# The first layer's normalisation of a two-layer trunk moved ahead of its first products

## The chip, the cores and the metric

One core of a Trainium2 chip runs one program for the whole trunk. TensorE is called PE below, VectorE DVE, ScalarE ACT, GpSimd POOL, and SyncE's queue, from which all the transfers are issued, SP. The metric is the device time of one execution in microseconds, as the median over several runs.

## What is computed

Two layers over 1024 positions of width 1024. Each normalises its input, scales and shifts it by a modulation that is worked out from a condition vector, multiplies it by one wide input matrix, runs three mixers over slices of the product, and merges their gated outputs. The change touches the lines down to `proj`, in the first layer.

```python
def rms_norm(x, g):
    x32 = x.astype(jnp.float32)
    y = x32 * lax.rsqrt(jnp.mean(x32 * x32, axis=-1, keepdims=True) + NORM_EPS)
    return (y * g).astype(x.dtype)
...
def hybrid_layer(x, c_act, positions, norm_g, w_ada, b_ada, w_in, ...):
    mod = c_act @ w_ada + b_ada
    shift, scale, gate = jnp.split(mod[:, None, :], 3, axis=-1)
    h = rms_norm(x, norm_g) * (1.0 + scale) + shift
    proj = h @ w_in
    pool_u, pool_g, q, k, v, ret_g, rw, rw_g, gate_logits = jnp.split(proj, points, axis=-1)
    o_pool = causal_pool_mixer(pool_u, pool_w, pool_scale) * jax.nn.silu(pool_g)
    o_ret = retention(q, k, v, positions, ret_norm_g) * jax.nn.silu(ret_g)
    o_rwkv = rwkv7_time_mix(rw, ...) * jax.nn.silu(rw_g)
    y = jnp.einsum('btnw,nwd->btnd', jnp.stack([o_pool, o_ret, o_rwkv], axis=2), w_branch)
    merged = jnp.sum(jax.nn.sigmoid(gate_logits.reshape(B, T, N_BRANCHES, D)) * y, axis=2)
    return x + gate * (merged @ w_out)
```

## The kernel before

The sequence stands on the free axis in two halves of 512 positions, `h` = 0 and 1. The width of 1024 stands on the partitions in eight row blocks, `kt` = 0 to 7. So the input is sixteen tiles of 128x512, `xin[h][kt]`. A product at full precision is made of three fast ones: both operands are split into a rounded part and a remainder (`hhi` and `hlo` for the inputs, `wh` and `wl`, or `wbig`, for the weights), and `mm1` issues hi by hi, lo by hi and hi by lo into one accumulator. A product of 128x512 of this kind is called a dense matmul below. One output tile of 128 columns over both halves takes 48 of them.

The modulation is 24 columns of 128 values: 0 to 7 are the shift, 8 to 15 the scale, 16 to 23 the gate. `ada` works out a group of them (`ADA`): for each of the eight row blocks of `w_ada` DVE multiplies a wide tile by one value of the condition and adds it to an accumulator in SBUF (L216, L218). PE then sums over the partitions with matmuls against a column of ones (`adaps`), and DVE adds the bias. For a scale group it also makes `acoef`, which is the norm's gain times one plus the scale. Before the change, the groups are 2, 2 and 4 columns of scale, then 4 and 4 of shift, then the gate.

The start is written out by hand, in one block in which the order of instructions on PE, DVE, ACT and POOL is that of the text (L1228 to L1343). It works in two passes:

1. The first three output tiles (`FIRST`: the lora columns, `k` and `r` of the first head pair) are multiplied from inputs that are only scaled (`scaled`: x times `acoef`, split into hi and lo). Their six accumulators stand in PSUM (`acc6`). They take 16 blocks of nine dense matmuls (`mms(h, kt)`), 144 in all. Beside that, ACT squares the inputs (`sq`), POOL sums the squares, and `rstd_task` makes the norm's factor for each position and spreads it over the partitions (`rbc`). The six products are multiplied by that factor when they leave PSUM (`first_raw`). What the shift contributes to them is worked out from a second load of the raw weights on DVE (`shift_bias`), and added at the end (`first_evac`).
2. For all further output tiles the inputs themselves are multiplied by the factor (`normed`, in place, on POOL and DVE), scaled and shifted (`shifted`), and split once more into the same hi and lo tiles. In this block the first two further output tiles, `v` of the first head pair and one of the pooling mixer, are multiplied as these tiles become ready.

After the block, a planner with its own clock (`wprep`, `pump`, `advance`) fills PE with the input tiles of the other mixers and places the steps of the mixers among them. The first matmul of a mixer's task is `lw` (L729), of the first head pair of the RWKV mixer. `FIRST` and `v` of that head pair must be out of PSUM before that task is added (L1045).

Transfers wait in SP's order; tiles of 256 KB follow one another with eight of them in flight.

Of the kernel before, what the change touches and what calls it, by code (L numbers as in the profile page):

```python
# [17 lines left out]
P = 128  # L18
# [71 lines left out]
def trunk_kernel(ctx, tc, xT, cvec, pos, vecs, consts, w_ada, w_all, pool_w, lora_w, out):  # L90
# [113 lines left out]
    def ada(l, g, slot_, gap=2200, acc_=t_lt, ws=None):  # L204
        c, n, _ = ADA[g]
        W_ = n * P
        acc = acc_("ada_acc")[:, 0:W_]
        late = ws is None
        ws = [] if late else ws
        for kt in range(NKT):  # L210
            i, o = divmod(kt * W_, HF)
            if late and o == 0:
                ada_load(l, g, slot_, ws, min(i + 2, 2 * n) - len(ws))
            w = ws[i][:, o : o + W_]
            if kt == 0:
                nc.vector.tensor_scalar_mul(acc, w, cact[:, 0:1])  # L216
            else:
                nc.vector.scalar_tensor_tensor(acc, w, cact[:, kt : kt + 1], acc, op0=ALU.mult, op1=ALU.add)  # L218
# [6 lines left out]
        o = VEC["b_ada"]  # L225
        nc.vector.tensor_tensor(mod[l][:, c : c + n], ps[:, 0:n], vec[l][:, o + c : o + c + n], op=ALU.add)
        if c >= 16:
            nc.vector.tensor_scalar_mul(mod[l][:, c : c + n], mod[l][:, c : c + n], 0.5)
        if 8 <= c < 16:
            o = VEC["norm_g"] + c - 8  # L230
            nc.vector.scalar_tensor_tensor(
                acoef[l][:, c - 8 : c - 8 + n], mod[l][:, c : c + n], 1.0, vec[l][:, o : o + n],
                op0=ALU.add, op1=ALU.mult,
            )
        yield
# [349 lines left out]
    def affine_hi(l, kt, x, res, eng=None):  # L585
        nc.scalar.activation(
            x, x, AF.Identity, bias=mod[l][:, kt : kt + 1], scale=acoef[l][:, kt : kt + 1]
# [381 lines left out]
    def shift_evac(l, mui, ps, h, am_prev, dst):  # L969
        o = VEC["mu_k"] + mui  # L970
        mu = vec[l][:, o : o + 1]
        keep = pin if pinned[0] else lambda i: i
        keep(nc.scalar.activation(dst[:, 1:HF], ps[:, 0 : HF - 1], AF.Copy, scale=mu))
        if h == 0:
            keep(nc.gpsimd.memset(dst[:, 0:1], 0.0))
# [26 lines left out]
    pinned = [False]  # L1002
# [18 lines left out]
    def evac_steps(item, ps, h, bias=None):  # L1021
        l, st, ams, lw = L_
        kind = item[0]
        if kind == "lora":
            d = mo("lt")
            ams["lora"] = shift_evac(l, 12, ps, h, ams.get("lora"), d)
            if bias:
                yield bias(d, h, 12)
# [4 lines left out]
        elif kind in ("k", "r", "v"):  # L1033
# [8 lines left out]
            if bias:  # L1042
                yield bias(d, h, mui)
# [45 lines left out]
    def evac(*a):  # L1089
        run(evac_steps(*a))  # L1090

# [12 lines left out]
    ssum = [None, None]  # L1104
    rbc = [[], []]
    wbig = []
    wparts = [[], [], []]
    acc6 = []

    sqs = {}  # L1110
# [7 lines left out]
    def sq(h, kt):  # L1118
        sqs[h, kt] = (mo if kt else t_cs)("sq")
        nc.scalar.square(sqs[h, kt], xin[h][kt])  # L1120
        if kt == 0:
            ssum[h] = sqs[h, kt]
        else:
            nc.gpsimd.tensor_tensor(ssum[h], ssum[h], sqs[h, kt], op=ALU.add)
# [17 lines left out]
    def scaled(h, *kts):  # L1142
        for kt in kts:
            x, a = xin[h][kt], acoef[0][:, kt : kt + 1]
            hi, lo = hb("hhi"), hb("hlo")
            nc.scalar.activation(hi, x, AF.Copy, scale=a)
            nc.vector.scalar_tensor_tensor(lo, x, a, hi.bitcast(F32), op0=ALU.mult, op1=ALU.subtract)
            h_cur[h].append((hi, lo))

# [4 lines left out]

    def rstd_copy(h):
        rb = t_lt("rbs")
        nc.scalar.copy(rb, rbc[h][0])
        rbc[h].append(rb)

    first_steps = []  # L1160

    raws = {}

    def first_raw(h, *tiles):
        for i in tiles:
            raws[h, i] = mo("raw")
            nc.vector.tensor_tensor(raws[h, i], acc6[h][i], rbc[h][1], op=ALU.mult)

    def first_evac(h, *tiles):
        for i in tiles:  # L1170
            st = evac_steps(FIRST[i], raws[h, i], h, lambda d, hh, mui, i=i: (d, hh, mui, i))
            first_steps.append((st, next(st)))

    def normed(eng, h, *kts):
        for kt in kts:
            eng.tensor_tensor(xin[h][kt], xin[h][kt], rbc[h][1], op=ALU.mult)

    def shifted(h, *kts):
        for kt in kts:
            x = xin[h][kt]  # L1180
            hi, lo = h_cur[h][kt]
            b, a = mod[0][:, kt : kt + 1], acoef[0][:, kt : kt + 1]
            if kt % 2 and (kt >= 4 or h):
                nc.scalar.activation(hi, x, AF.Identity, bias=b, scale=a)
                nc.vector.tensor_scalar(x, x, a, b, op0=ALU.mult, op1=ALU.add)
            else:
                nc.scalar.activation(x, x, AF.Identity, bias=b, scale=a)
                nc.scalar.copy(hi, x)
            nc.vector.tensor_tensor(lo, x, hi.bitcast(F32), op=ALU.subtract)

    def shift_bias():
        ws = [[None, None] for _ in range(3)]
        for i in range(3):
            for j in range(2):
                ws[i][j] = wada_slot("wraw")
                nc.sync.dma_start(out=ws[i][j], in_=w_all[0, i, j])
        yield
        acc = t_cs("bacc")
        for i in range(3):
            ai = acc[:, i * P : (i + 1) * P]  # L1200
            for kt in range(NKT):
                w = ws[i][kt // 4][:, kt % 4 * P : kt % 4 * P + P]
                b = mod[0][:, kt : kt + 1]
                if kt == 0:
                    nc.vector.tensor_scalar_mul(ai, w, b)
                else:
                    nc.vector.scalar_tensor_tensor(ai, w, b, ai, op0=ALU.mult, op1=ALU.add)
        ps = mx("bias")
        for i in range(3):
            mmul(ps[:, i : i + 1], acc[:, i * P : (i + 1) * P], ones)  # L1210
        b = t_cs("bias")[:, 0:3]
        nc.vector.tensor_copy(b, ps[:, 0:3])
        for st, (d, h, mui, i) in first_steps:
            bi = b[:, i : i + 1]
            if h == 0:
                nc.vector.scalar_tensor_tensor(
                    d[:, 0:1], bi, omu[0][:, mui : mui + 1], d[:, 0:1], op0=ALU.mult, op1=ALU.add
                )
                nc.scalar.activation(d[:, 1:HF], d[:, 1:HF], AF.Identity, bias=bi)
            else:  # L1220
                nc.scalar.activation(d, d, AF.Identity, bias=bi)
            run(st)
# [5 lines left out]
    with tc.manual_schedule(engines={ET.PE, ET.DVE, ET.Activation, ET.Pool}):  # L1228
        acc6.append([acc_ps() for _ in range(3)])
        acc6.append([ps_c.tile([P, HF], F32, tag=t, name=nm("acc"), bufs=n) for t, n in (("cy", 2), ("cy", 2), ("ch", 1))])  # L1230
        aw = [[] for _ in range(5)]
        gs = [ada(0, g, None, acc_=t_vp if g == 4 else t_lt, ws=aw[g]) for g in range(5)]
# [3 lines left out]

        aload(0, 4)
        nc.sync.dma_start(out=vec[0], in_=vecs[0])
        wdma(0, 0)
        wsp(0, 0)  # L1240
        xdma(0, 0, 1)
        wdma(0, 1, 2)
        xdma(1, 0, 1)
        aload(1, 4)
        xdma(0, 2, 3)
        xdma(1, 2, 3)
        steps(gs[0], 9)
        derive(0)
        scaled(0, 0)
        wsp(0, 1)  # L1250
        steps(gs[1], 3)
        scaled(0, 1)
        wsp(0, 2)
        steps(gs[1], 5)
        mms(0, 0, 1)
        sq(0, 0)
        sq(0, 1)
        steps(gs[1], 1)
        scaled(1, 0, 1)
        sq(1, 0)  # L1260
        sq(1, 1)
        mms(1, 0, 1)
        aload(2, 8)
        for h in range(2):
            for kt in (2, 3):
                steps(gs[2], 2)
                scaled(h, kt)
                sq(h, kt)
        mms(0, 2, 3)
        wdma(1, 0, 1, 2)  # L1270
        xdma(0, 4, 5, 6, 7)
        nc.sync.dma_start(out=cst, in_=consts[:, 0 : CST["bone"]])
        xdma(1, 4, 5, 6, 7)
        wsp(1, 0, 1, 2)
        mms(1, 2)
        steps(gs[2], 1)
        mms(1, 3)
        for tag in ("wh", "wl"):
            for _ in range(3):
                w = wp.tile([P, HF], F32, tag=tag, name=nm("wada"), bufs=3)  # L1280
                ada_load(0, 3, lambda _: w, aw[3], 1)
        aload(3, 2)
        for kt in range(4, 8):
            sq(0, kt)
            scaled(0, kt)
            mms(0, kt)
        for kt in range(4, 8):
            sq(1, kt)
            scaled(1, kt)
            steps(gs[3], 2)  # L1290
        wprep(True)
        aload(4, 8)
        r0 = rstd_task([ssum[0]], rbc[0])
        r1 = rstd_task([ssum[1]], rbc[1])
        mms(1, 4)
        next(r0)
# [26 lines left out]
        for i in range(2):  # L1323
            pss[i, 0] = acc_ps()
# [330 lines left out]
```

## Time and profile before

| | |
|---|---|
| median of 3 runs | 2525.3 us (2524.45 to 2537.53) |
| the profiled execution | 2538.0 us, span 2536.3 us |
| mean granted TensorE clock | 0.971 |
| PE, DVE, ACT, POOL busy | 95%, 55%, 31%, 33% of the span |
| moved by DMA | 225 MB, mean 89 GB/s |

A row of the timeline gives the start in the span, the busy time, the engine, the line and operation, and the tiles as written by read, with what ended the idle time before it in brackets. Rows of groups give the total and the mean duration of one. The duration of a matmul is longer than the step from one to the next, as they are pipelined; so the step between starts is what counts. Matmuls on fp32 operands appear twice in the trace, since each is made in two passes.

### The profile page before, as it was taken

Reading aid. Unit: us, or ns where it says so; the run is one execution under the profiler, and the core shown is the slowest. Engines: PE = TensorE matmul, PEld = TensorE weight load, DVE = VectorE, ACT = ScalarE, POOL = GpSimd, SP = SyncE. Lnnn points to the kernel's source line nnn. Section 1 sums busy time; section 2 is a strip of 40 time slices with the busy share of each in tenths; the row PEclk is TensorE's granted clock in tenths of the full one; section 3 lists DMA queues with packets and bytes.
Section 4 is the critical chain, followed back from the end, with each engine's and each line's share of the span. In section 5 each row is a group of like instructions: output and inputs, shape, how many; then the busy total and the mean of one; then the engine's idle time right before and its main releaser. Section 6 shows DMA issues by size and latency. Waiting matters only on the chain. (4 is left out here: it accounts for less than half of the span.)

```text
span 2536.3 us, 34936 instructions
## 1 busy us (share of the span) xinstructions
PE 2417.6 (95%) x13318; PEld 1995.5 (79%) x13318; DVE 1394.0 (55%) x2588; ACT 796.6 (31%) x1482; POOL 847.6 (33%) x729
## 2 busy tenths in 40 slices
PE   6889999999899999999999999999999999999998
PEld 4677887787788788877878787788878778787888
DVE  7886358357547935267455735844744663412344
ACT  4642232233224222212353223223322322221243
POOL 5522223133133332364452222322313322236441
PEclk9799999999999999999999999999999989999999
DMA  6222112011112413666541211211211121354342
GB/s 229 76 88 71 38 38 84 28 40 64 55 35 83 133 47 130 189 212 195 170 126 34 80 34 38 68 41 35 86 45 38 60 79 51 117 158 122 105 152 76
DMA packets 125080, 225.25 MB, mean 89 GB/s; under 512 B 14192, under 2 KB 17520, under 8 KB 124912
## 3 DMA queue, kind: packets, MB, share of 16 engines
q1 hardware_dynamic: 124912, 223.01, 27.8%
q8 instruction: 105, 1.72, 0.3%
q14 instruction: 63, 0.52, 0.1%
HBM read 176.03 MB, written 46.92 MB: 88 GB/s over the span
## 5 line engine op out<-in xcount | busy, mean ns | idle before, releaser
L513 POOL TENSOR_TENSOR wl<-wr,wh 128x512 fp32r<-128x512 f32 x338 | 450.3, 1333 | 1220.2 <-ACT wh L512 1123.0
L394 PE MATMUL acc<-hhi,wh 128*128 128x512 f32 x1968 | 799.5, 406 | 29.1 <-DVE k L981 29.1
L394 PE MATMUL acc<-hlo,wh 128*128 128x512 f32 x1968 | 801.7, 407 | 0.0
L394 PE MATMUL acc<-hhi,wl 128*128 128x512 f32 x1968 | 799.2, 406 | 0.0
L394 PEld LDWEIGHTS acc<-hhi,wh 128*128 128x128 f32 x1968 | 377.7, 192 | 100.4 <-DVE k L981 31.6
L512 ACT CAST wh<-wr 128x512 fp32r<-128x512 f32 x338 | 209.3, 619 | 734.3 <-PE acc L394 476.0
L394 PEld LDWEIGHTS acc<-hhi,wl 128*128 128x128 f32 x1968 | 377.6, 192 | 68.8 <-issue 2.2
L394 PEld LDWEIGHTS acc<-hlo,wh 128*128 128x128 f32 x1968 | 377.2, 192 | 68.8 <-issue 1.3
L394 PE MATMUL acc<-olo,wh 128*128 128x512 f32 x384 | 154.2, 402 | 5.8 <-POOL olo L513 5.8
L394 PE MATMUL acc<-oG,wh 128*128 128x512 f32 x384 | 153.1, 400 | 3.5 <-ACT oG L512 1.7
L394 PE MATMUL acc<-oG,wl 128*128 128x512 f32 x384 | 152.5, 398 | 0.0
L936 DVE SCALAR_TENSOR_TENSOR S<-ch,pc,SP 64x64 f32<-64x64 f32 x256 | 72.5, 283 | 105.0 <-PE ch L394 98.5
L925 DVE TENSOR_TENSOR xst<-cy,MT 64x128 f32<-64x128 f32 x128 | 36.1, 282 | 168.7 <-PE cy L394 168.4
L922 ACT ACTIVATE SP<-S,pc 128x128 f32<-128x128 f32 x128 | 51.4, 402 | 179.1 <-DVE S L936 175.1
L858 DVE TENSOR_TENSOR tm<-MT 64x30 f32<-64x30 f32 (+14 forms) x240 | 100.2, 417 | 7.6
L864 DVE TENSOR_TENSOR MT<-MT,tm 64x30 f32<-64x30 f32 (+14 forms) x240 | 95.2, 397 | 7.8
L931 DVE COPY Z<-ch 64x128 f32<-64x128 f32 x128 | 36.1, 282 | 112.3 <-PE ch L394 111.7
L394 PEld LDWEIGHTS acc<-olo,wh 128*128 128x128 f32 x384 | 73.2, 191 | 24.6 <-POOL olo L513 8.9
L394 PEld LDWEIGHTS acc<-oG,wh 128*128 128x128 f32 x384 | 73.2, 191 | 22.7 <-ACT oG L512 2.9
L1482 DVE SCALAR_TENSOR_TENSOR gs<-gs,acc 128x512 f32<-128x512 f32 x64 | 43.5, 682 | 85.8 <-PE acc L394 74.6
L218 DVE SCALAR_TENSOR_TENSOR ada_acc<-wada,cact,ada_acc 128x512 f32<-128x512 f32 (+1 forms) x68 | 70.0, 1029 | 31.9 <-DMA wada<-in_w_ada 31.0
L394 PEld LDWEIGHTS acc<-oG,wl 128*128 128x128 f32 x384 | 73.6, 192 | 16.6
(292 smaller groups left out, 3825.3 us busy)
## 6 DMA issues: line engine op xcount, KB each, us to landing
wr<-in_w_all SPq DMA_DIRECT2D x364, 256.0 KB, 2.7
gd<-gsg SPq DMA_DIRECT2D x80, 256.0 KB, 2.0
gs<-gd SPq DMA_DIRECT2D x80, 256.0 KB, 2.9
wada<-in_w_ada SPq DMA_DIRECT2D x70, 256.0 KB, 3.0
ol<-od SPq DMA_DIRECT2D x64, 256.0 KB, 2.9
ringG<-in_w_ada SPq DMA_DIRECT2D x26, 256.0 KB, 5.3
x<-in_xT SPq DMA_DIRECT2D x16, 256.0 KB, 5.4
od<-po SPq DMA_DIRECT2D x16, 256.0 KB, 2.1
```

The source lines that it names most:

```text
L218: nc.vector.scalar_tensor_tensor(acc, w, cact[:, kt : kt + 1], acc, op0=ALU.mult, op1=ALU.add)
L394: nc.tensor.matmul(out, lhsT=lhsT, rhs=rhs, start=start, stop=stop, **kw)
L512: nc.scalar.copy(hi, src)
L513: eng.tensor_tensor(lo, src, hi.bitcast(F32), op=ALU.subtract)
L858: nc.vector.tensor_tensor(pr, M3[:, i + 1 :, i : i + 1].to_broadcast([64, n, i]), M3[:, i : i + 1, 0:i].to_broadcast([64, n, i]), op=ALU.mult,
L864: nc.vector.tensor_tensor(M3[:, i + 1 :, 0:i], M3[:, i + 1 :, 0:i], pr, op=ALU.add)
L922: nc.scalar.activation(SP, S, AF.Copy, scale=pcc)
L925: nc.vector.tensor_tensor(xst[0:64, :], cy[0:64, 0:P], AV[:, c * P : (c + 1) * P], op=ALU.add)
L931: nc.vector.tensor_copy(Z[0:64, c, :], ch[0:64, 0:P])
L936: nc.vector.scalar_tensor_tensor(Sn[rw, rw], ch[rw, P + 64 * hd : P + 64 * hd + 64], pc[rw, c : c + 1], SP[rw, rw], op0=ALU.mult, op1=ALU.add,
L1482: nc.vector.scalar_tensor_tensor(s, s, 1.0, ps, op0=ALU.add, op1=ALU.mult)
```

## The change

The whole first layer's input is normalised first, then scaled and shifted and split once, and only then multiplied.

- `ADA` is regrouped by row block: a group holds the scale columns and the shift columns of the same row blocks (one block in each of the groups 0 to 3, two in 4 and 5), then the gate. `SHIFT` says where each shift column now stands in `mod`. The order holds for the second layer too.
- The groups 0 and 1 are made on PE alone (`ada_pe`): 16 matmuls of 128x1 each, with the modulation's weights as the stationary operand. The groups 2 to 5 stay on DVE, but their partial sums stand in PSUM until the last step.
- Squares are added in pairs on DVE and summed over the partitions by PE (`sq2`). The factor's spread copy stays in PSUM for DVE (`rbc`), with a copy in SBUF (`rbs`) for the four tiles that POOL normalises.
- `affine` lets ACT make hi and the full value from the normalised tile, both with scale and bias; `low` subtracts, on DVE or POOL. Each input tile is made once.
- `scaled`, `first_raw`, `first_evac`, `shifted`, `shift_bias`, the second load of six raw weight tiles and the biases in the evacuation go. The six accumulators are evacuated by the same code as all others.
- `v` of the first head pair and the tile after it leave the hand-written block and are multiplied in the planner's loop, where an accumulator's both halves are filled in turn. All sixteen x tiles are loaded ahead of weights and modulation.

```diff
-for _c, _k in ((8, 2), (10, 2), (12, 4), (0, 4), (4, 4), (16, 4), (20, 4)):
-    ADA.append((_c, _k, _n))
-    _n += 2 * _k
+SHIFT, SCALE = {}, {}
+for _c, _k in ((0, 1), (1, 1), (2, 1), (3, 1), (4, 2), (6, 2)):
+    _o = sum(len(a[1]) for a in ADA)
+    for _i in range(_k):
+        SCALE[_c + _i], SHIFT[_c + _i] = _o + _i, _o + _k + _i
+    ADA.append((_c, [8 + _c + _i for _i in range(_k)] + [_c + _i for _i in range(_k)], _n))
+    _n += 4 * _k
...
+        part = acc if late else mx("ada_ps")[:, 0:W_]
...
-                nc.vector.tensor_scalar_mul(acc, w, cact[:, 0:1])
+                nc.vector.tensor_scalar_mul(part, w, cact[:, 0:1])
             else:
-                nc.vector.scalar_tensor_tensor(acc, w, cact[:, kt : kt + 1], acc, op0=ALU.mult, op1=ALU.add)
+                nc.vector.scalar_tensor_tensor(
+                    part if kt < NKT - 1 else acc, w, cact[:, kt : kt + 1], part, op0=ALU.mult, op1=ALU.add
+                )
...
+    def ada_pe(l, g, ws):
+        n = len(ADA[g][1])
+        W_ = n * P
+        ps = mx("adaps")
+        for kt in range(NKT):
+            i, o = divmod(kt * W_, HF)
+            for m in range(n):
+                mmul(
+                    ps[:, m : m + 1], ws[i][:, o + m * P : o + (m + 1) * P], cact[:, kt : kt + 1],
+                    start=(kt == 0 and m == 0), stop=(kt == NKT - 1 and m == n - 1), skip_group_check=True,
+                )
+            yield
+        ada_end(l, g, ps)
+        yield
...
+    def sq2(h, j):
+        a, b = mo("sq"), t_lt("sq")
+        nc.scalar.square(a, xin[h][2 * j])
+        nc.scalar.square(b, xin[h][2 * j + 1])
+        nc.vector.tensor_tensor(a, a, b, op=ALU.add)
+        if j == 0:
+            ssp[h] = mx("ssps")
+        for m in range(4):
+            mmul(
+                ssp[h][:, m : m + 1], a[:, m * P : (m + 1) * P], ones,
+                start=(j == 0 and m == 0), stop=(j == 3 and m == 3), skip_group_check=True,
+            )
...
+    def rstd(h):
+        rn = sp.tile([P, 4], F32, tag="rn", name=nm("rn"))
+        nc.scalar.activation(rn, ssp[h][:, 0:4], AF.Sqrt, bias=eps_n, scale=1.0 / D)
+        nc.vector.reciprocal(rn, rn)
+        rn_[h] = rn
...
+    def normed(h, *kts, pool=False):
+        for kt in kts:
+            x = xin[h][kt]
+            if pool:
+                nc.gpsimd.tensor_tensor(x, x, rbs[h], op=ALU.mult)
+            else:
+                nc.vector.tensor_tensor(x, x, rbc[h], op=ALU.mult)
+
+    def affine(h, kt):
+        x = xin[h][kt]
+        b, a = mod[0][:, SHIFT[kt] : SHIFT[kt] + 1], acoef[0][:, kt : kt + 1]
+        hi, lo = hb("hhi"), hb("hlo")
+        nc.scalar.activation(hi, x, AF.Identity, bias=b, scale=a)
+        nc.scalar.activation(x, x, AF.Identity, bias=b, scale=a)
+        h_cur[h].append((hi, lo))
+
+    def low(eng, h, kt):
+        hi, lo = h_cur[h][kt]
+        eng.tensor_tensor(lo, xin[h][kt], hi.bitcast(F32), op=ALU.subtract)
...
+        xdma(0, *range(8))
+        nc.sync.dma_start(out=cst, in_=consts[:, 0 : CST["bone"]])
+        nc.sync.dma_start(out=vec[0], in_=vecs[0])
+        xdma(1, *range(8))
+        wdma(0, 0)
         aload(0, 4)
-        nc.sync.dma_start(out=vec[0], in_=vecs[0])
-        wdma(0, 0)
+        wdma(0, 1)
+        aload(1, 4)
+        wdma(0, 2)
...
+        rstd_bc(1)
+        normed(0, 6, 7, pool=True)
         steps(gs[0], 9)
+        aload(3, 2)
+        normed(1, 0)
+        affine(0, 0)
+        normed(1, 1)
+        low(V, 0, 0)
         wsp(0, 1)
+        affine(1, 0)
+        normed(1, 2)
+        low(V, 1, 0)
+        steps(gs[1], 9)
+        wdma(1, 0, 1, 2)
+        aload(4, 6)
+        affine(0, 1)
+        normed(1, 3)
         wsp(0, 2)
+        low(V, 0, 1)
+        affine(1, 1)
+        normed(1, 4, 5, 6, 7)
+        low(G_, 1, 1)
+        acc6[0] = [acc_ps() for _ in range(3)]
         mms(0, 0, 1)
+        acc6[1] = [ps_c.tile([P, HF], F32, tag=t, name=nm("acc"), bufs=n) for t, n in (("ch", 1), ("cy", 2), ("cy", 2))]
+        mms(1, 0)
+        steps(gs[2], 9)
+        affine(0, 2)
+        low(G_, 0, 2)
+        affine(1, 2)
+        low(G_, 1, 2)
+        mms(1, 1)
+        wsp(1, 0)
+        mms(0, 2)
+        steps(gs[3], 9)
...
+        for _ in range(8):
+            steps(gs[4], 1)
+            aload(5, 1)
+        steps(gs[4], 1)
+        affine(0, 4)
+        low(V, 0, 4)
+        affine(1, 4)
+        low(G_, 1, 4)
         mms(1, 3)
+        affine(0, 5)
+        low(V, 0, 5)
+        affine(1, 5)
+        low(G_, 1, 5)
+        mms(0, 4)
+        mms(1, 4)
+        mms(0, 5)
+        steps(gs[5], 9)
+        affine(0, 6)
+        low(V, 0, 6)
+        affine(0, 7)
+        low(V, 0, 7)
+        mms(1, 5)
+        affine(1, 6)
+        low(G_, 1, 6)
+        affine(1, 7)
+        low(V, 1, 7)
         wprep(True)
...
+        wprep()
+        mms(0, 6, 7)
+        mms(1, 6, 7)
     seen[0] = len(nc.cur_bb.bb.instructions)
+    L_ = (0, {}, {}, [])
+    L_[3].extend(lora_load(0))
+    for i in range(3):
+        evac(FIRST[i], acc6[0][i], 0)
+    for i in range(3):
+        evac(FIRST[i], acc6[1][i], 1)
     wprep()
```

More of the change, by code (lines that the diff above doesn't have):

```diff
@@ L1001, in trunk_kernel @@
     L_ = None
-    pinned = [False]
     def enter_layer(l):
@@ L1174, in normed @@
[L1174 to L1222, printed above, removed]
@@ L1228, in trunk_kernel @@
     with tc.manual_schedule(engines={ET.PE, ET.DVE, ET.Activation, ET.Pool}):
[L1229 to L1232, printed above, removed]
+        V, G_ = nc.vector, nc.gpsimd
+        aw = [[] for _ in range(6)]
+        gs = [(ada_pe if g < 2 else ada)(0, g, ws=aw[g], **({} if g < 2 else dict(slot_=None))) for g in range(6)]
@@ L1256, in trunk_kernel @@
[L1256 to L1274, printed above, removed]
@@ L1292, in trunk_kernel @@
[L1292 to L1296, printed above, removed]
-        mms(1, 5)
-        run(r0)
-        rstd_copy(0)
-        steps(gs[3], 1)
-        steps(gs[4], 2)
-        for i in range(3):
-            first_raw(0, i)
-            steps(gs[4], 1)
-        normed(nc.gpsimd, 0, 0, 1, 2, 3, 4, 5, 6, 7)
-        mms(1, 6)
-        next(r1)
-        steps(gs[4], 1)
-        shifted(0, 0)
-        steps(gs[4], 1)
@@ new lines, in trunk_kernel @@
+        mms(1, 0)
[8 more added lines that the diff above has]
+        steps(gs[3], 9)
+        aload(4, 2)
+        affine(0, 3)
+        low(G_, 0, 3)
+        affine(1, 3)
+        low(G_, 1, 3)
+        mms(1, 2)
+        mms(0, 3)
+        wsp(1, 1, 2)
+        for _ in range(8):
[3 more added lines that the diff above has]
+        affine(0, 4)
```

184 lines of the change are left out of this document (60 added, 124 removed).

## The prediction, made before the changed kernel ran

> **What bounds the kernel now.** The page first, for the span, the busiest engine and where it is less busy; then stages of the span.
>
> ```profile
> span 2536.3 us, 34936 instructions
> PE 2417.6 (95%) x13318; PEld 1995.5 (79%) x13318; DVE 1394.0 (55%) x2588; ACT 796.6 (31%) x1482; POOL 847.6 (33%) x729
> PE   6889999999899999999999999999999999999998
> ...
> PEclk9799999999999999999999999999999989999999
> ```
> ```profile
> 0.00:127.00 127.00, 93.64 (x357) 72.70 (x358) 105.93 (x159) 66.35 (x111) 66.43 (x57) 0.85 0.44 152
> 127.00:250.00 123.00, 110.25 (x563) 88.08 (x562) 94.93 (x164) 42.24 (x70) 29.01 (x26) 0.94 0.26 82
> 250.00:400.00 150.00, 146.73 (x908) 122.08 (x907) 76.48 (x166) 50.65 (x102) 41.71 (x39) 1.00 0.13 41
> ```
>
> The columns of the stages are the stretch, its length, busy time and count on PE, weight loads, DVE, ACT and POOL, the granted clock and DMA. PE bounds the kernel: from 250 us on it is nearly always at work at full clock. Only the start has a hole: in the first 127 us PE is busy for 93.6, and at 0.85 of its clock. So a change in the start is worth the PE time that it wins or loses there, up to a point from which both kernels run dense. I take the first matmul of the RWKV task, `lw`, and count the dense matmuls ahead of it.
>
> ```profile
> L394 PE MATMUL acc<-hhi,wbig 128*128 128x512 f32 x128 | 50.8, 471 | 3.7 <-ACT hhi L1188 2.3 <-ACT hhi L1146 1.5
> L394 PE MATMUL acc<-hlo,wbig 128*128 128x512 f32 x64 | 31.2, 487 | 13.8 <-DVE hlo L1147 7.1 <-DVE hlo L1189 6.7
> ...
> L394 PE MATMUL acc<-hhi,wh 128*128 128x512 f32 x26 | 10.2, 393 | 0.0
> L394 PE MATMUL acc<-hlo,wh 128*128 128x512 f32 x25 | 9.8, 393 | 0.0
> L394 PE MATMUL acc<-hhi,wl 128*128 128x512 f32 x25 | 9.7, 389 | 0.0
> ```
> ```profile
> 110.00 0.39 PE L394 MATMUL acc<-hlo,wh 128*128 128x512 f32 x1
> ...
> 115.21 0.39 PE L394 MATMUL acc<-hhi,wh 128*128 128x512 f32 x1
> ...
> 121.97 0.50 PE L394 MATMUL lw<-lt,lw 64*128 64x512 f32 x1
> ```
>
> The groups are those of the first 122 us: 128 + 64 + 26 + 25 + 25 = 268 dense matmuls. The timeline has 23 steps between 110.00 and 115.21, so one takes 0.2265 us at full clock. They need 60.7 us; `lw` comes at 121.97; 61.3 us are lost. In the order of the changed kernel 193 of them (144 + 48 of `v` + 1) stand ahead of `lw`. The other 75 are not saved but come behind it: 75 x 0.2265 = 17.0 us. The break-even is therefore `lw` at 121.97 - 17.0 = **105.0 us**. The rest of the prediction is when the changed kernel gets there.
>
> **The change, part by part.** Durations of the steps:
>
> ```profile
> 9.07 1.01 PE L394 MATMUL adaps<-fixed,ada_acc 128*128 128x1 f32 x4 [9.07 <-DVE ada_acc L218]
> ...
> 9.45 1.26 POOL L513 TENSOR_TENSOR wbig<-wr,wbig 128x512 fp32r<-128x512 f32 x1 [8.23 <-ACT wbig L512]
> ...
> 11.54 0.80 PE L394 MATMUL acc<-hhi,wbig 128*128 128x512 f32 x1 [1.45 <-ACT hhi L1146]
> ...
> 18.47 0.50 PE L394 MATMUL acc<-hlo,wbig 128*128 128x512 f32 x1 [1.94 <-DVE hlo L1147]
> ...
> 40.65 1.07 PE L394 MATMUL adaps<-fixed,ada_acc 128*128 128x1 f32 x8
> ...
> 63.12 2.05 PE L394 MATMUL rbc<-cst,rn 128*128 128x128 f32 x8 [5.65 <-issue]
> 64.96 1.71 PE L394 MATMUL adaps<-fixed,ada_acc 128*128 128x1 f32 x8
> ...
> 67.10 0.63 PE L394 MATMUL acc<-hlo,wbig 128*128 128x512 f32 x1
> ...
> 68.38 0.63 PE L394 MATMUL acc<-hlo,wbig 128*128 128x512 f32 x1
> ...
> 70.51 1.70 PE L394 MATMUL ssps<-fixed,sq 128*128 128x1 f32 x8
> ```
> ```profile
> L1120 ACT ACTIVATE sq<-x 128x512 f32<-128x512 f32 x16 | 9.7, 616 | 0.1
> L1187 ACT ACTIVATE x<-x,mod,acoef 128x512 f32<-128x512 f32 x10 | 8.1, 807 | 11.3 <-DVE mod L226 8.1 <-DVE x L1176 3.2
> ...
> L1167 DVE TENSOR_TENSOR raw<-acc,rbs 128x512 f32<-128x512 f32 x6 | 4.1, 676 | 0.0
> ...
> L513 POOL TENSOR_TENSOR wbig<-wr,wbig 128x512 fp32r<-128x512 f32 x8 | 12.3, 1562 | 9.6 <-ACT wbig L512 9.6
> ...
> L218 DVE SCALAR_TENSOR_TENSOR ada_acc<-ringG,cact,ada_acc 128x512 f32<-128x512 f32 x16 | 20.9, 1309 | 0.2
> ```
> ```profile
> 30.00:40.00 10.00, 5.76 (x20) 4.00 (x19) 9.23 (x8) 0.00 (x0) 6.64 (x4) 0.87 1.05 387
> x<-in_xT SPq DMA_DIRECT2D x16, 256.0 KB, 5.4
> ```
>
> *Removed:* `scaled`, a second split of 16 tiles, six products with the factor, `shift_bias`. All of it is DVE, ACT and POOL work in the first 122 us. It hides behind nothing, since DVE is the engine that PE waits for there (7.1 + 6.7 us on `hlo` above), but it pays only through an earlier `lw`.
>
> *The squares and factors.* At 387 GB/s a tile of 256 KB takes 0.68 us and lands 5.4 us after its issue; the eighth x tile is there at about 10.5 us. Two squares, a DVE sum and 8 passes (1.70 us at half clock) for each pair: PE ends the first half's sums at about 14.0. The second half's squares stand on ACT behind the first factor (14.3). Its four PE blocks with the first spread (2.05) between them end at 26.5, its own factor and spread at **29.1**.
>
> *The modulation on PE.* `ada_pe` twice is 2 x 16 matmuls in two passes, 64 passes. Row 64.96 gives 0.214 us a pass at half clock, row 40.65 0.134 at full clock. PE will have had nothing but such small work, so I take 0.214: 13.7 us, and the first dense matmul at **42.8**, against 11.54 before. The weights do not wait: the last tile of these groups is about the 27th transfer, at 24 us. This is the price of the change. Bounds: 0.134 and, from row 9.07 (1.01 / 4), 0.25: -5.1 to +2.3 us here, and about as much again on the sums and spreads before it.
>
> *Blocks 1 to 3* (27 dense). At half clock a step is (68.38 - 67.10) / 3 = 0.427 us. Hi by lo of the third tile waits for `wsp(0, 2)`, which ACT copies behind two `affine` steps, and POOL ends at about 47. The clock comes up after some 7 us, as between the first dense matmul (11.54, 0.80 long) and that at 18.47 (0.50); so they end at **53.3**.
>
> *Groups 2 and 3 of the modulation* are 8 steps of 256 columns each on DVE, partial sums in PSUM. No row writes PSUM from DVE. The nearest is L1167, which reads one operand there: 0.676 us for 512 columns, at work while POOL runs, where L218 with both operands in SBUF has 1.309. I take 0.73 in a chain of dependent steps, and 0.48 for 256 columns; bounds 0.61 and 1.31. PE takes the results in order between blocks. Coefficients, `affine` (0.81 + 0.81) and `low` on POOL (1.26 in row 9.45, 1.56 on average) make PE wait 1 to 1.5 us in each of the two blocks (0, 2) and (0, 3); group 3 leaves PE at **59.7**.
>
> *Groups 4 and 5* on DVE: 8 x 0.73 = 5.8 us each. Group 4 runs from 60.2 to 66.1 beside dense work; PE waits for its eight passes and the first `affine` until about 70. Group 5 cannot start before `low(0, 5)`, at 73.1, and ends at 79.0; its passes end at **80.0**, where 45 dense matmuls are left. These need 10.2 us at full clock and 3 more if the pause has taken the clock down for its first half. With 0.7 us for a remainder, the 144 end at **91 to 94**; `v` takes 48 x 0.2265 = 10.9; `lw` comes at 102 to 105, and I take **103.5**. If the DVE chain in PSUM costs 1.31 a step, 9 us are added; if 0.61, 2 come off.
>
> *SP and POOL queues.* The six x tiles that now stand ahead of weights delay nothing that PE could use earlier. Loads for group 5 wait on SP for group 4's steps and land at 70, ahead of 73.1. Evacuation: three accumulators of half 0 are done four microseconds before `v` needs one, so ACT (0.7) and DVE (0.74) are hidden by blocks (1, 6) and (1, 7).
>
> *After `lw`.* Before, DVE was still at work on shift and rotary tables when the RWKV task began:
>
> ```profile
> PE nps L394 <- DVE ksl L759: 4.0, 2, 2.4
> PE bt L400 <- DVE BK L795: 0.8, 1, 0.8
> PE lw L394 <- DVE lt L513: 0.7, 1, 0.7
> ```
>
> These waits (122 to 165 us) come to 5.5 us. In the new order the rotary steps stand behind the first half's preparation on DVE. I take 3.5 of the 5.5 as won; bounds 0 and 5.5.
>
> *Sum* against the profiled execution: (103.5 - 105.0) - 3.5 = **-5 us**, 2538.0 to 2533. That execution is 12.7 us above the median of the runs shown, so against the median it is 2525.3 - 5 = **2520 us**.
>
> **Rivals.** *PE is warm during the small matmuls.* The Trainium skill (page "TensorE: Matmul & The Clock Gate", part 1) says that the clock doubles after about 3.4 us of sustained matmul activity; read so, 13.7 us of back-to-back `ada_pe` would run at full clock. Against it speak the rows above: 63.12 to 66.67 is filled with small matmuls, and the dense ones at 67.10 and the small ones at 70.51 are still at half clock. For it, no stretch of before has small ones alone for so long. At 0.134 a pass everything up to 42.8 comes 9.5 us earlier: 2510 us.
>
> *The RWKV chain bounds the layer.* Then not dense work but an earlier `lw` counts: -18.5 us, 2507. Against it: PE is busy 146.73 of 150 us beside that chain.
>
> *The clock stays down through the new start, slower than before.* From 53 to 94 us PE takes modulation sums in order between blocks and waits for `affine` and `low` behind each. In these rows waits of that kind cost the clock:
>
> ```profile
> 60.00:70.00 10.00, 6.88 (x24) 6.22 (x25) 6.21 (x11) 0.58 (x1) 4.13 (x3) 0.57 0.26 79
> ...
> 80.00:90.00 10.00, 5.47 (x16) 3.77 (x16) 10.00 (x13) 1.28 (x2) 8.67 (x9) 0.59 0.19 60
> 90.00:100.00 10.00, 7.71 (x21) 5.94 (x22) 10.00 (x22) 6.74 (x11) 1.74 (x1) 0.55 0.09 26
> ```
>
> If the 117 dense matmuls after block 3 all run at half clock they cost 117 x 0.2 = 23 us more, of which the waits (two of 1 to 1.5, about 3 before group 5, about 3 before block (0, 4)) take up some 8: +15, 2535. It decides where PE's busy share falls to that of the second row, 5.5 of 10. For it: the two waits of 3 us. Against it: a block lasts 2 us and the other waits about 1.
>
> **How the numbers follow.** Forecast 0.57 (2520, own range 2511 to 2529, from the DVE step and the pass), warm PE 0.12 (2510), RWKV chain 0.10 (2507), clock down 0.21 (2535). The range takes in both ends: 2505 to 2538. 0.5%, or 12.6 us, is about what a measurement of this kernel can tell from no change. Faster than 2512.7: most of two rivals (0.16) and a sixth of the forecast (0.09), 0.25. Slower than 2537.9: half of the last rival (0.11), and 0.05 for a forecast with the DVE step and the pass both at their upper bounds and nothing won after `lw`. Within: 0.59.
>
> **What would show it.** First dense matmul at 42.8 (33 if PE is warm). `adaps` of group 5 at 79 to 80. `lw` at 103.5 with 193 dense ahead of it; a time that moves without `lw` moving by as much, 17.0 us counted, would prove the break-even wrong. Granted clock over 0.85 between 54 and 94. Steps of the partial sums in PSUM of 0.48 and 0.73 us, whatever POOL does. Waits of `nps`, `bt` and `lw` under 2 us in all.

## The result, and the profile after

The changed kernel takes 2523.3 us (median of 20 runs, 2512.8 to 2531.6). Beside it the kernel before takes 2536.2 us (median of 20, 2524.5 to 2545.4), so the median of the three runs that the prediction had lies at the low end of these. The ratio is 0.9949, 95% interval 0.9937 to 0.9962: the change wins 13 us. In the experiment b_gate_k below, the longest of six times, 2539.9 us, counts in the median and not in the ratio. The forecast of 2520 us is met, but from a base of 2525.3 it stood for a gain of 5 us. So the question is where the other 8 us come from. The profiled execution after the change takes 2522.4 us, with a span of 2520.6.

First the stages of the span after, with the columns of the prediction (stretch, length, busy time and count on PE, weight loads, DVE, ACT and POOL, granted clock, DMA).

```profile
0.00:127.00 127.00, 107.98 (x459) 90.63 (x460) 67.62 (x126) 64.88 (x102) 36.78 (x45) 0.97 0.42 141
127.00:250.00 123.00, 117.58 (x718) 94.31 (x717) 83.13 (x152) 43.10 (x72) 28.03 (x24) 0.99 0.28 86
250.00:400.00 150.00, 146.51 (x814) 122.34 (x814) 91.56 (x188) 48.37 (x97) 46.07 (x43) 0.99 0.14 44
```

DVE is freed as the diff promises (67.62 us in place of 105.93 in the first stretch), and PE works more. But the start is not where the time is won. The timeline of PE after gives the steps that the prediction named:

```profile
30.05 13.65 PE L425 MATMUL adaps<-cact,ringG 128*128 128x1 f32 x64
43.56 0.77 PE L425 MATMUL acc<-hhi,wbig 128*128 128x512 f32 x1
...
80.02 1.84 PE L425 MATMUL adaps<-fixed,ada_acc 128*128 128x1 f32 x8 [3.06 <-DVE ada_acc L226]
81.72 0.77 PE L425 MATMUL acc<-hhi,wbig 128*128 128x512 f32 x1
...
105.56 0.49 PE L425 MATMUL lw<-lt,lw 64*128 64x512 f32 x1
```

`lw` comes at 105.56, and the break-even was 105.0: the start loses 0.6 us. All of the gain comes behind it. In the stretch from 127 to 1250 us, which is the rest of the first layer, PE is idle for 47.2 us before (1123 - 1075.81) and for 37.0 us after (1123 - 1086.00), and the granted clock is 0.99 in place of 0.98. That stage before, and then after:

```profile
127.00:1250.00 1123.00, 1075.81 (x6011) 885.78 (x6010) 651.74 (x1212) 329.45 (x620) 366.54 (x309) 0.98 0.30 94
```
```profile
127.00:1250.00 1123.00, 1086.00 (x6084) 894.50 (x6083) 646.13 (x1213) 329.76 (x619) 370.68 (x313) 0.99 0.31 96
```

The waits of PE there (us in total, times, longest) say why. Before:

```profile
PE acc L394 <- DVE k L981: 18.2, 3, 6.4
PE nps L394 <- DVE ksl L759: 5.2, 4, 2.4
PE rot L400 <- DVE yc L658: 4.6, 3, 2.1
```

After:

```profile
PE rot L431 <- DVE yc L689: 12.8, 7, 3.7
PE acc L425 <- ACT gsg L1084: 5.8, 2, 5.2
PE nps L425 <- DVE bv L871: 2.8, 1, 2.8
```

The largest wait of the layer, three stops of some 6 us in front of a dense matmul, is gone. The timeline of the kernel before shows the first of the three, on DVE and then on PE:

```profile
230.84 1.97 DVE L868 STREAM_TRANSPOSE MT<-MT 32x1024 f32<-32x1024 f32 x1
232.71 3.75 DVE L873 STREAM_TRANSPOSE G<-MT 32x1024 f32<-32x1024 f32 x2
236.49 1.41 DVE L981 SCALAR_TENSOR_TENSOR k<-acc,omu,k 128x512 f32<-128x512 f32 x2
...
237.30 0.80 PE L394 MATMUL acc<-hhi,wh 128*128 128x512 f32 x1 [6.12 <-DVE k L981]
```

The `k` tile of the next head pair fills an accumulator, and DVE must empty it (L981). In DVE's order that instruction stands behind the long block with which the RWKV task of the head pair before inverts its small matrices, and the three transposes at the end of that block last 5.7 us. Until they are over, PE has no free accumulator. The same three transposes in the changed kernel:

```profile
218.56 2.22 DVE L899 STREAM_TRANSPOSE MT<-MT 32x1024 f32<-32x1024 f32 x1
220.66 4.00 DVE L904 STREAM_TRANSPOSE G<-MT 32x1024 f32<-32x1024 f32 x2
```

Here PE is multiplying gate tiles, which ACT evacuates alone, and does not stop. The code of this part is the same in both kernels. What has moved is the RWKV task against the tiles: `lw` is 16.4 us earlier, and one tile of the pooling mixer stands behind it. Which of the two took the stops away is not shown.

### The profile page after: what moved, and what is told of

It is laid out like the page before. It is cut to its first block, busy times and chain, and to the rows that moved or that the text cites. A ratio compares the mean times of both kernels' runs of the same rounds, so it can differ in the third digit from the quotient of the medians.

```text
span 2520.6 us, 35022 instructions
## 1 busy us (share of the span) xinstructions
PE 2425.8 (96%) x13416; PEld 2007.9 (80%) x13416; DVE 1345.5 (53%) x2548; ACT 792.1 (31%) x1465; POOL 815.7 (32%) x715
## 5 line engine op out<-in xcount | busy, mean ns | idle before, releaser
L425 PE MATMUL acc<-hhi,wh 128*128 128x512 f32 x2000 | 809.4, 405 | 16.8 <-DVE k L1011 11.0
L425 PE MATMUL acc<-hhi,wl 128*128 128x512 f32 x2000 | 810.7, 405 | 1.7 <-POOL r L1005 1.7
L425 PE MATMUL acc<-hlo,wh 128*128 128x512 f32 x2000 | 811.7, 406 | 0.0
L425 PEld LDWEIGHTS ch<-xst,G 128*128 128x128 f32 x512 | 76.7, 191 | 11.6 <-DVE xst L956 0.5
```

What stands on the lines that cost most here:

```text
L425: nc.tensor.matmul(out, lhsT=lhsT, rhs=rhs, start=start, stop=stop, **kw)
```

## The experiments

Theory A: the gain is the three stops before `k`, which the change avoids by a shift of the order. Theory B, the rival of the prediction which the numbers alone favour: the layer follows the RWKV chain, so the 16.4 us by which `lw` is earlier become the 13. In the table `lw` is that of the profiled execution, and the ratio is to the kernel before on the same chip.

| run | median us | ratio, 95% interval | lw at |
|---|---|---|---|
| changed kernel | 2523.3 | 0.9949, 0.9937 to 0.9962 | 105.6 |
| b_gate_k | 2511.9 | 0.9902, 0.9869 to 0.9936 | 121.2 |
| b_kfree | 2484.6 | 0.9803, 0.9772 to 0.9835 | 120.1 |
| a_kfree | 2505.4 | 0.9880, 0.9838 to 0.9921 | 106.7 |
| a_gate_k2 | 2534.7 | 0.9990, 0.9967 to 1.0014 | 104.9 |
| a_gate_v | 2543.0 | 1.0029, 1.0010 to 1.0047 | 117.1 |
| a_ada_twice | 2528.8 | 0.9985, 0.9966 to 1.0005 | 120.5 |
| a_v2 | 2507.5 | 0.9903, 0.9872 to 0.9935 | 99.4 |
| a_k_pu | 2511.7 | 0.9896, 0.9855 to 0.9936 | 115.1 |
| a_v2k_pu | 2512.3 | 0.9900, 0.9868 to 0.9932 | 110.0 |
| b_nopool_k | 2508.4 | 0.9876, 0.9843 to 0.9909 | 120.7 |
| a_warm (one time) | 2512.5 | | 106.1 |
| a_sbuf (one time) | 2518.5 | | 109.7 |

**The stops before k, moved away in the kernel before.**

```diff
 def plan_layer(l):
...
                 if done < 4:
+                    if l == 0:
+                        early[l].add(pre[0])
+                        yield pre.popleft()
                     yield from RW(done)
```

> The kernel before, with one gate tile (48 dense matmuls, about 10.9 us of PE) put ahead of the k tile of head pairs 1 to 3 in the first layer; the number of matmuls is the same. Theory A (a meeting on DVE): in the first layer of the kernel before, PE stops for 6.1, 5.7 and 6.4 us because a k tile, which DVE must help to evacuate, comes due while DVE works at the transposes of the RWKV task; a gate tile is evacuated by ACT alone, so the three stops (18.2 us) go, and with them three stretches at half clock of some 3 us each. Less what new stops take: 10 to 27 us faster than before, 2509 to 2526. Theory B (the RWKV chain bounds the layer, so that an earlier lw made the change faster): each later head pair starts up to 10.9 us later, so it is 11 to 33 us slower, 2547 to 2569.

It takes 2511.9 us, 24 us less than the kernel before (25 by the ratio) and 11 less than the changed one, with the old start and `lw` where it was. That is in the range of theory A, and theory B has the wrong sign. The waits of PE from 127 to 1250 us have no `k` any more; the longest are now:

```profile
PE pps L394 <- DVE pdl L516: 7.2, 2, 4.7
PE acc L394 <- POOL olo L516: 5.2, 3, 2.9
```

**The stops taken away at their cause, in both kernels.** `k` and `r` leave PSUM through ACT, so that no order can put them behind DVE's block. The diff is the same in both.

```diff
 def shift_evac(l, mui, ps, h, am_prev, dst, free=False):
+        if free:
+            t = mo("kt")
+            nc.scalar.activation(t, ps, AF.Copy, scale=omu[l][:, mui : mui + 1])
+            nc.gpsimd.tensor_tensor(dst, dst, t, op=ALU.add)
+        else:
...
-            ams[item] = shift_evac(l, mui, ps, h, ams.get(item), d)
+            ams[item] = shift_evac(l, mui, ps, h, ams.get(item), d, kind in ('k', 'r') and i > 0)
```

> The kernel before, with the k and r tiles of head pairs 1 to 3 evacuated from PSUM by ACT alone (two scaled copies, added on POOL), so that their accumulators no longer wait behind the transposes on DVE; both layers, start and order of tiles as before. Theory A (PE's stops before k, and the half-clock stretches behind them, are what the two kernels differ by): the stops of 6.1, 5.7, 6.4 us in the first layer and 4.1, 4.3, 2.6 us in the second go, 29 us, and up to 3 us of half clock behind each; less new stops: 18 to 45 us faster than before, 2491 to 2518. Theory B (the RWKV chain bounds the layer): the chain is no shorter, so 0 to 5 us faster.

> The changed kernel with the same evacuation by ACT and POOL. Theory A: its first layer has no stops before k, its second has 4.0, 4.2 and 2.8 us; so less is to be won than in the kernel before: 11 us and up to 3 us of half clock for each, 6 to 20 us faster than the changed kernel, 2503 to 2517. Theory B: no change, 2523.

The changed kernel, at 2505.4 us, lies where theory A put it. The kernel before, at 2484.6, is 6 us faster than theory A allowed. The stops before `k` were the first row of its waits over the whole span:

```profile
PE acc L394 <- DVE k L981: 29.1, 6, 6.4
```

In both runs that row is gone. The edit is worth 1.97% in the kernel before (50 us over both layers), and 0.69% in the changed kernel (17 us), which has such stops in its second layer only. Not all of this is the stops: the edit also takes work off DVE, and behind the last `lw`, where no `k` follows, PE's idle time falls from 19.9 to 13.0 us in the one and from 20.1 to 13.0 in the other. The two run the second layer in the same order. So the difference, 1.28% or some 32 us (give or take 13 by the intervals), is what the change avoids in its first layer. That is more than the 13 us that it wins. Once the stops are gone the change makes the kernel slower, 0.9880 against 0.9803 or about 20 us, with intervals that just do not meet. The kernel before with this edit is the fastest of all that ran.

**The same shift in the second layer.**

```diff
 def plan_layer(l):
...
                 if done < 4:
+                    if l == 1:
+                        early[l].add(pre[0])
+                        yield pre.popleft()
                     yield from RW(done)
```

> The changed kernel, with one gate tile put ahead of the k tile of head pairs 1 to 3 in the second layer alone, which both kernels run in the same order with stops of 4.0, 4.2 and 2.8 us before k. Theory A: these 11 us and three stretches at half clock go, less what new stops take: 6 to 20 us faster than the changed kernel, 2503 to 2517. Theory B: 11 to 33 us slower, 2534 to 2556.

A miss: 11 us slower, at the near edge of what theory B said. The waits of its second layer show that the stops shrank, from 11.0 us to

```profile
PE acc L425 <- DVE k L1014: 5.0, 2, 3.2
```

and stages of the same execution show where more was lost:

```profile
1640.00:1667.00 27.00, 27.00 (x190) 20.50 (x189) 0.75 (x1) 6.07 (x11) 1.44 (x2) 0.50 0.04 10
...
1856.00:1889.00 33.00, 33.00 (x231) 25.20 (x232) 1.25 (x3) 6.56 (x12) 1.44 (x2) 0.50 0.11 32
```

PE is busy all the time at half its clock, for 27 and 33 us, which at full clock would be half as long. In both stretches blocks of small matmuls of the RWKV task (32x32 and 64x64) alternate with two to five dense ones; each begins within some 2 us of a stop, of 1.8 and 3.2 us, and each ends in a longer row of dense matmuls. In the kernel before, where dense matmuls alone follow the stop at 237.30, the half clock lasts 4.9 us. So what follows a stop seems to decide what it costs in all: some 2.4 us more in front of dense work, and over 13 us more here. That the stop starts such a stretch is not shown; below is one without a stop ahead.

**lw later, with the same work.**

```diff
-        yield from [("lora",)] + RW(0)
+        yield from [("lora",)] + RW(0)[:2]
+        if l == 0:
+            early[l].add(("gate", 0, 0))
+            yield ("gate", 0, 0)
+        yield ("v", 0)
...
```

The gate tile is left out at its later place.

> The changed kernel, with one gate tile put ahead of v of the first head pair, so lw comes 10.9 us later (at about 116.5) and the same work follows it less those 48 matmuls. Theory A (work is conserved, only PE's stops count): within 6 us of the changed kernel's 2523. Theory B (the layer follows lw): 11 us slower, 2534.

It is 20 us slower, more than either theory said. The profiled execution, one of the fastest of this run, is 10.6 us behind that of the changed kernel. It has 22 us at a clock of 0.51 in its third head pair, again among blocks of small matmuls and behind a stop:

```profile
660.00:682.00 22.00, 22.00 (x128) 16.80 (x126) 1.03 (x2) 4.67 (x8) 1.28 (x1) 0.51 0.08 25
```

The changed kernel loses time in the same place too, but less: over this head pair the clock is 0.95 there (181.5 us) and 0.92 here (188.1 us), which makes some 6 us of the 10.6. The rest was not traced further. The run does not speak for B alone, since a later `lw` also shifts the task against the tiles.

**Does start time reach the end?** Two runs change the start and leave all that follows in its order. One makes the 64 passes twice:

```diff
 def ada_pe(l, g, ws):
-        for kt in range(NKT):
+        for kt in range(2 * NKT):
...
```

> The changed kernel, with the 64 passes of the modulation on PE made twice (the first time into a PSUM tile that nobody reads). All that follows keeps its order. Both theories: the first dense matmul and lw come 13.7 us later and so does the end, 2535 to 2537. If the small passes were hidden behind something else, under 5 us.

`lw` moves by 14.9 us in the profiled execution, as it should. The median moves by only 5.5, with times from 2523.9 to 2547.4; by the ratios it is 9 us, give or take 6. So the forecast of the full 13.7 us is missed by the median, and by the ratios just not ruled out. The other shortens the start:

```diff
+        steps(gs[1], 8)
         steps(gs[0], 9)
...
         affine(0, 4)
-        low(V, 0, 4)
+        low(G_, 0, 4)
+        steps(gs[5], 8)
...
-        steps(gs[5], 9)
+        steps(gs[5], 1)
```

Besides, group 1 is made by `ada` in place of `ada_pe`, and `low(0, 5)` goes to POOL.

> The changed kernel with a shorter start: the second modulation group is summed on DVE, which is idle from 26 to 37 us, in place of 32 passes on PE (6.8 us; 0.9 remain), and the sixth group on DVE comes right behind the fifth, at 68 in place of 73.6, with two more remainders on POOL. All that follows the start keeps its order. First dense matmul at 38.5 to 39.5, the pause of 3.1 us at 77 to 80 under 1 us, lw at 95 to 99 in place of 105.6. If start time reaches the end as it is: 6 to 10 us faster than the changed kernel, 2513 to 2517. If what the layer gives back depends on where stops fall against the small matmuls, the first 150 us gain as much but the end may lie anywhere within 10 us of that.

The first dense matmul is at 38.50 and `lw` at 99.35, 6.2 us earlier (a little short of the forecast); the kernel takes 2507.5 us, 16 less than the changed one (12 by the ratios) and under the 2513 to 2517 that start time alone would give. Its trace splits that. One matmul far into the second layer stands in the changed kernel and in a_v2 at

```profile
2036.08 0.80 PE L425 MATMUL pps<-pdl,pw 128*128 128x512 f32 x1 [2.91 <-DVE pdl L544]
```
```profile
2031.58 0.80 PE L425 MATMUL pps<-pdl,pw 128*128 128x512 f32 x1 [2.58 <-DVE pdl L544]
```

which is 4.5 us earlier: so far three quarters of the 6.2 us have come through. The other 10 us of the profiled execution come in the next 50 us. The stages of the changed kernel, and then of a_v2:

```profile
2062.00:2074.00 12.00, 12.00 (x114) 9.27 (x110) 0.00 (x0) 2.32 (x4) 0.00 (x0) 0.54 0.14 45
2074.00:2086.00 12.00, 12.00 (x64) 9.09 (x64) 0.00 (x0) 3.42 (x6) 0.08 (x1) 0.50 0.01 1
```
```profile
2055.00:2079.00 24.00, 24.00 (x263) 19.50 (x263) 1.70 (x6) 8.03 (x15) 2.56 (x2) 1.00 0.14 45
```

The same blocks of small matmuls, with the same dense ones between them, run at half clock in one execution and at full clock in the other, and in the slower one PE does not stop in the 25 us ahead of them. So start time reaches the end in part at least; how much of it is not settled by these two runs, as one such stretch moves the time by some 10 us either way.

**Small passes and the clock.** Twenty dense matmuls on data that nobody needs:

```diff
+                nc.tensor.matmul(
+                    wps, lhsT=wt[:, 0:P], rhs=wt, start=True, stop=True
+                )
...
+        warm(12)
         wsp(0, 0)
         rstd_bc(1)
```

> The changed kernel with 20 matmuls of 128x512 more, on data that nobody needs, into a PSUM tile that nobody reads: 4, 4 and 12 of them among the sums of the second half, ahead of the 64 passes of the modulation on PE. If PE's clock is raised by such matmuls and small passes hold it once raised, the 64 passes take 8.6 us (0.134 each) in place of 13.65. If small passes do not hold the clock, they take 13.65 again. The 12 put up to 3 us on PE's path; lw at 103 to 106 in the first case, at 107 to 109 in the second.

Neither case came true as it stands. The timeline has the passes at

```profile
29.64 4.33 PE L1242 MATMUL acc<-wt 128*128 128x512 f32 x12
33.81 1.05 PE L425 MATMUL rbc<-cst,rn 128*128 128x128 f32 x8
34.70 9.44 PE L425 MATMUL adaps<-cact,ringG 128*128 128x1 f32 x64
```

and three stages of these passes alone (length, PE busy and count, then weight loads, DVE, clock, DMA) show how the 9.44 us come about:

```profile
34.70:37.70 3.00, 3.00 (x28) 3.00 (x28) 0.00 (x0) 1.00 0.32 84
37.70:40.70 3.00, 3.00 (x23) 3.00 (x22) 0.16 (x1) 0.77 0.55 178
40.70:43.70 3.00, 3.00 (x16) 3.00 (x15) 0.00 (x0) 0.50 0.14 29
```

The dense matmuls raise the clock, 28 passes fit into 3 us, and some 5 us later, with PE filled by passes, the clock falls to half and 16 fit. `lw` comes at 106.05, so the start wins nothing by it.

**Partial sums in SBUF.**

```diff
-        part = acc if late else mx("ada_ps")[:, 0:W_]
+        part = acc
```

> The changed kernel with the partial sums of the modulation on DVE in SBUF in place of PSUM. The steps took 0.785 us for 512 columns in PSUM; in SBUF, beside POOL, 1.31 as in the kernel before: 16 steps of 512 columns and 16 of 256 columns, of which the 16 wide ones add 8.4 us; lw 6 to 10 us later, at 112 to 116. If it is the chain of dependent steps and not the memory that sets the 0.785: lw within 2 us of 105.6.

Half a miss. `lw` comes at 109.73, 4.2 us later in place of 6 to 10. The groups of DVE give the steps (total, mean ns), of this run and then of the changed kernel:

```profile
L226 DVE SCALAR_TENSOR_TENSOR ada_acc<-ringG,cact,ada_acc 128x512 f32<-128x512 f32 x14 | 15.0, 1074 | 0.5
```
```profile
L226 DVE SCALAR_TENSOR_TENSOR ada_ps<-ringG,cact,ada_ps 128x512 f32<-128x512 f32 x12 | 9.1, 756 | 0.4
```

PSUM is worth 0.32 us a step here, not 0.55.

**Where the other 20 us lie.** Without stops before `k`, the changed kernel is about 20 us behind the kernel before. In the runs that follow, too, `k` and `r` leave PSUM through ACT. First, the tile of the pooling mixer put back ahead of `v`, with the start as changed and as shortened:

```diff
-        yield from [("lora",)] + RW(0)
+        yield from [("lora",)] + RW(0)[:2]
         pools = deque(PL(i) for i in range(4))
+        if l == 0:
+            yield pools[0].pop(0)
+        yield ("v", 0)
```

> The changed kernel with k and r evacuated by ACT and POOL, and with the first tile of the pooling mixer put back ahead of v of the first head pair, as in the kernel before; so lw comes 10.9 us later, at about 117, with 241 dense matmuls ahead. The two kernels without stops before k stand at 2484.6 (before) and 2505.4 (changed), though the count of dense matmuls puts their starts level. Theory A2 (the rest is the order: how the RWKV steps fall against the tiles of the other mixers): with the tiles as before the 21 us come back, 2480 to 2492. Theory B (the layer follows lw): 11 us slower than 2505, 2516. Theory D (the start costs more than the count says, order does not matter): 2505.

> The same with the shorter start (second modulation group on DVE, sixth group earlier), which brought lw from 105.6 to 99.3. If start time reaches the end as it is: 6 to 8 us faster than the run beside it, 2473 to 2486 by theory A2; it would then beat the kernel before with k and r evacuated by ACT and POOL (2484.6).

2511.7 and 2512.3 us: the order as before does not bring the time back, and theory A2 falls in this form. One reason stands in the timeline of a_k_pu, a new stop of the same make:

```profile
140.70 0.79 PE L425 MATMUL acc<-hhi,wh 128*128 128x512 f32 x1 [7.45 <-DVE silu L1056]
```

The second pooling tile also needs DVE to leave PSUM, and DVE is at the RWKV preparation and the rotary tables. In the second run the shorter start (`lw` at 110.0 in place of 115.1) does not show at all, which fits the scatter above but no theory.

Last, the kernel before with the tile taken out of its start:

```diff
         wprep()
-        first.append(wready.popleft())
...
-        for j in range(2):
-            mm3(pss[1, 0], first[1][1][j], h_cur[0][4 * j : 4 * j + 4], j == 0, j == 1)
...
```

> The kernel before with k and r evacuated by ACT and POOL, and with the first tile of the pooling mixer taken out of the hand-written start, so that it is multiplied behind the start of the RWKV task, as in the changed kernel; the start is otherwise that of the kernel before, the number of matmuls the same. 48 dense matmuls (10.9 us) go behind lw, which comes at 110 to 117. With the tile ahead the kernel stands at 2484.6; the changed kernel without stops before k at 2505.4. If the 21 us between these come from the order (pooling tile behind lw), this run lies at 2497 to 2510, though lw is earlier. If they come from the changed start itself, it lies at 2480 to 2490. If the layer followed lw, at 2474 to 2480.

2508.4 us, in the range of the order theory; but `lw` did not come earlier (120.71 against 120.08). Dense matmuls of the next tiles took the place of most of those that were moved: 257 stand ahead of `lw`, against 268. By the prediction's count the start has thus lost 11 x 0.2265 = 2.5 us, plus 0.6 for `lw`. Against b_kfree the run is 24 us slower (18 by the ratios), so most of this is the order, or scatter that comes with it.

The traces say in what form. These are the stages from `lw` to the `lw` of the second layer, of b_kfree, b_nopool_k and a_kfree:

```profile
120.08:1317.40 1197.32, 1168.60 (x6486) 964.88 (x6485) 700.52 (x1277) 386.38 (x717) 429.23 (x363) 0.99 0.31 97
120.71:1346.50 1225.79, 1190.48 (x6499) 974.32 (x6498) 689.03 (x1276) 387.82 (x718) 422.55 (x364) 0.98 0.31 97
106.72:1345.40 1238.68, 1198.90 (x6563) 987.90 (x6562) 699.58 (x1287) 388.61 (x717) 426.19 (x366) 0.98 0.30 94
```

The last is 41.4 us longer than the first. 17.0 of that are the 75 dense matmuls that the change moved behind `lw`; of the other 24, 11.1 are more idle time of PE (39.8 against 28.7), and most of the rest goes with the lower clock. So in these executions the loss lies in other waits and more half clock in the first layer. That the order of the tiles alone causes it, and how much of it is scatter, stays open.

## Why the prediction was right or wrong

- **The start, right.** First dense matmul at 43.56 (42.8 forecast), the passes 13.65 us (13.7), group 5's passes at 80.02 (end forecast at 80.0), `lw` at 105.56 (103.5). The term came to +0.6 in place of -1.5; the 2 us went into a pause of 3.06 and the half clock behind it.
- **DVE in PSUM, right.** 0.756 us for 512 columns (0.73 forecast) and 0.490 for 256 (0.48). The price of doing without was overrated, 9 us against 4.2.
- **Warm PE, wrong rival.** The 64 passes stayed at 0.213 us each.
- **Clock down, wrong rival.** From 54 to 94 us the granted clock was 0.91.
- **After lw, the failed step.** The prediction took "3.5 of the 5.5 as won; bounds 0 and 5.5", from the waits between 122 and 165 us. In that place it erred little: from 105.56 to 150 us PE is busy for 44.44 of 44.44 us, so all 5.5 are won. The term was too small because the window ended too early. The profile of before had, in its waits of PE over the whole span, a first row of 29.1 us in six stops before `k`; it was not asked what the new order does to them. Three of the six went, worth some 32 us, and other waits and half clock gave back some 20.
- **The break-even** counts work rightly, but not what its place does. That was the test named in the prediction, a time that moves without `lw`: in b_gate_k `lw` moves by 0.7 us and the time by 24, in b_kfree by 1.9 and 50.
- **The RWKV chain as bound.** `lw` 16.4 us earlier and 13 us won looks like this rival, and b_gate_k and b_kfree rule it out as the cause. a_gate_k2 came out where this rival had it and a_gate_v beyond it; the traces show half clock there, for a_gate_v only in part.
- **The base.** The gain was put at 5 us and is 13; the base was 10.9 us low. The two nearly cancel, so that 2520 is met by chance as much as by reason.

## What to carry to other kernels

Where PE is 95% busy, look first at the few waits that stop it and at what stands ahead of the releasing instruction on its engine; here an edit of a few lines, which took away six stops behind long DVE blocks, won nearly four times what the whole rewrite of the start did. A change that moves work between stages shifts everything behind it against everything else, so its effect on such meetings has to be read from the profile of before over the whole layer, not only near the change. And test the reason on the kernel before: an improvement that goes away once an unrelated stop is mended was not the change's own.

## What the runs showed of the hardware

Small matmuls did not raise PE's clock here, and did not always hold it. 64 passes of 128x1 in a row left it at half for 13.65 us, and raised beforehand it fell again some 5 us into them. Stretches in which blocks of 32x32 and 64x64 matmuls alternate with a few dense ones ran at half for 22 to 33 us with PE never idle; one such stretch ran at 1.00 for 24 us in a_v2. The Trainium skill (page "TensorE: Matmul & The Clock Gate", part 1) says that the warm-up is a matter of time, about 3.4 us of sustained activity, and not of the number of matmuls. For dense matmuls the trace has a time of that order, 5 us from 43.6 on; for the 128x1 passes it shows no rise in 13.65 us, and the measurement decides.

The granted clock of a stage can read 1.00 where PE runs at half. In the changed kernel these are the 64 passes alone, 16 in 3 us as in the last stage of a_warm above:

```profile
33.00:36.00 3.00, 3.00 (x16) 3.00 (x15) 0.00 (x0) 1.00 0.72 208
36.00:39.00 3.00, 3.00 (x16) 3.00 (x15) 0.16 (x1) 1.00 0.10 40
```

In a_warm the same passes went 28 to 3 us under a column of 1.00. So in the start, ahead of the first fall that it shows, the column does not tell the low clock; the step between like matmuls does.
